# A planner that is told TensorE's measured times, and first loads that are let through one behind the other

## The chip, the cores and the metric

The kernel runs on one core of a Trainium2 chip. The metric is the device time of one execution in microseconds; the kernel before takes 572.33 us (median of 3 runs, 572.28 to 572.41). The core has TensorE (PE: matmuls into PSUM, and PEld, its weight loads), VectorE (DVE), ScalarE (ACT), GpSimd (POOL) and SyncE (SP), which here issues every DMA. Each engine works through its own list of instructions in order and waits on semaphores for the others.

## The reference

Two decoder layers on x of 256 positions by 1024 channels, all in float32. Layer 0 mixes positions with a gated MLP, layer 1 with attention (one block of 256 keys, so it is plain causal attention with a relative-position bias); after each stands a gated ConvFFN of width 2816, and each sub-layer ends in a LayerNorm of alpha * x + f(x).

```python
def chunked_gmlp(x, w_in, ln_g, ln_b, w_s, b_s, w_out):
    z = jax.nn.gelu(x @ w_in)
    u, v = jnp.split(z, 2, axis=-1)
    v = layer_norm(v, ln_g, ln_b)
    ...
    sv = jnp.einsum('gts,bnsgc->bntgc', w, v) + b_s.T[None, None, :, :, None]
    return (u * sv.reshape(B, S, GMLP_WIDTH)) @ w_out

def conv_ffn(x, w_up, conv_w, conv_b, w_down):
    h = x @ w_up
    ...
    g, val = jnp.split(hc, 2, axis=-1)
    return (jax.nn.gelu(g) * val) @ w_down

def reference(...):
    for i in range(DEPTH):
        ...
        x = layer_norm(DN_ALPHA * x + y, ln_mix_g[i], ln_mix_b[i])
        y = conv_ffn(x, f_w_up[i], f_conv_w[i], f_conv_b[i], f_w_down[i])
        x = layer_norm(DN_ALPHA * x + y, ln_ffn_g[i], ln_ffn_b[i])
    return x
```

## The kernel before

Weights stream from HBM in chunks of 128 rows by 2048 columns (1 MB): the v half of the gMLP's input projection (a_v, 4 chunks), its u half (a_u, 4), a_out (4), f_up0 (22), f_dn0 (11), b_v (4), b_qk (8), b_o (4), f_up1 (22) and f_dn1 (11). A float32 product is made of three faster ones: each weight w is split into whi (ACT copies it into the rounded type float32r) and wlo = w - whi (DVE subtracts), the activations likewise into the two parts of xt, and PE adds up x_hi*whi, x_hi*wlo and x_lo*whi. `prep(i)` loads chunk i into one of two buffers `raw` and splits it; `whi` and `wlo` are rings of ten halves, so five chunks are split ahead (CHUNKS = 5). Once a chunk's matmuls are recorded, `spent` calls `prep` for the chunk five further on.

The first stage, a_v in `gmlp()`, needs per step k (128 of the 1024 input channels) half a chunk of a_v and the columns k of the transposed input, which come as "xT" and are split into xt. Its 8 steps have 12 matmuls of 512 columns each: two blocks of positions t, two halves of 512 outputs p, three products. Steps 0 to 3 take both t in turn; then t = 0 does k = 4 to 7, and t = 1 after it. The table FIRST cuts the first two chunks' loads into pieces with a rank, and XFIRST gives the pieces of xT theirs; a rank is the load's place in SP's order, 0 to 8. Chunks 2 and 3 have none and reuse the buffers of chunks 0 and 1.

```
    FIRST = {0: [(0, 512, 0), (512, 1024, 2), (1024, 2048, 4)], 1: [(0, 1024, 6), (1024, 2048, 7)]}
    XFIRST = ((0, 1, 1), (1, 1, 3), (2, 2, 5), (4, 4, 8))
```

After a_v come gelu and a LayerNorm of v (`stats`, `scaled`), then a_u with the mixing matmuls `spatial(g)` laid between its own, then a_out.

No order is written out by hand. Every operation is recorded in a `Plan` with a cost in ns, its inputs and outputs. `emit` computes due times back from PE's list and then plays the engines against each other with these costs (line 122 on): PE's main work ("bulk") keeps the recorded order; its other work ("fill": transposes, spatial, the attention's scores and products) goes in as soon as the plan says that its inputs are there. The engines' lists are what this play gives. The costs of a matmul stand in `mms` (line 322) and those of transposes in line 333: 216 ns for a float32r matmul of 512 columns, 109 for one of 256.

`project_out` does a_out, f_dn and b_o: their last TAIL = 6 steps go position block by position block, and within t = 0 half by half (p0 with all its steps, then p1). When a half is complete DVE adds it to x (`add`, line 612) and takes statistics; then the mean, the power on POOL and one scaling per half (line 351) make the normalised x that PE transposes (line 332) for the next stage, while the matmuls of t = 1 go on.

## Time and profile before

| | |
|---|---|
| median of 3 runs | 572.33 us |
| the profiled execution: its time, its span | 571.2 us, 569.5 us |
| PE busy | 556.1 us (98%) |
| DVE busy | 464.3 us (82%) |
| ACT busy | 359.2 us (63%) |
| DMA | 110.9 MB, mean 195 GB/s |

The span runs from the first to the last instruction of the profiled execution; the run's time has 1.7 us around it, and the median lies 1.1 us above this one run. An engine is busy while it executes. Matmuls are pipelined, so their busy times overlap and their pace is read from the distance between their starts. The waits say which engine waited for which, and the chain of waits follows the work back from the last instruction.

### The profile page before, as it was taken

The numbers are of one execution on the slowest core, as the hardware profiler recorded it, in microseconds if no ns is written. First come the engines' busy times: TensorE is split into PE (matmuls) and PEld (weight loads), VectorE is DVE, ScalarE is ACT, GpSimd is POOL, SyncE is SP. The second block draws the span as 40 slices with busy tenths as digits, with TensorE's granted clock in tenths as the row PEclk, the third lists the DMA queues.
The fourth block names the chain that finished last, engine by engine and source line by source line (L and its number), as shares of the span: only waits on it lengthen the run. The fifth ranks groups of instructions, "written<-read, shape, count | busy, mean of one in ns | idle before, by whom it ended". The sixth has DMA issues, their size and how long they took to land.

```text
span 569.5 us, 8289 instructions
## 1 busy us (share of the span) xinstructions
PE 556.1 (98%) x3098; PEld 474.9 (83%) x3098; DVE 464.3 (82%) x873; ACT 359.2 (63%) x652; POOL 11.5 (2%) x17
## 2 busy tenths in 40 slices
PE   6999999999999999999999999999999999999994
PEld 4799888888888878888888877788888888888884
DVE  5598989999999997467958988579989999996526
ACT  5555558776777686335578877377777767775300
POOL 0020010000000000001000000010000000000001
PEclk9999999999999999999999999999999999999998
DMA  7897435547554577742665653506455556566302
GB/s 266 330 361 283 181 146 182 189 153 279 171 211 155 216 229 266 270 165 74 222 221 185 194 210 115 222 2 221 156 218 219 201 174 218 195 242 229 147 1 74
DMA packets 20132, 110.92 MB, mean 195 GB/s; under 512 B 2251, under 2 KB 6268, under 8 KB 7676
## 3 DMA queue, kind: packets, MB, share of 16 engines
q1 hardware_dynamic: 20092, 110.39, 54.2%
q8 instruction: 24, 0.39, 0.3%
q14 instruction: 16, 0.13, 0.1%
HBM read 109.31 MB, written 1.07 MB: 194 GB/s over the span
## 4 chain that ended last, share of the span: by engine, by line
PE 95%; DMA 2%; DVE 1%; SPq 0%; ACT 0%; issue 0%; DVEq 0%
PE twos L326 52%; PE bank L326 41%; DMA raw<-in_a_v 2%; PE bank L332 1%; PE twos L332 1%; DVE wlo L344 0%; DVE x L348 0%; SPq L355 0%; ACT whi L338 0%; DVE stat L494 0%; DVEq L966 0%; DVE stat L497 0%; DVE stat L499 0%; DVE xt L344 0%
## 5 line engine op out<-in xcount | busy, mean ns | idle before, releaser
L344 DVE TENSOR_TENSOR wlo<-raw,whi 128x1024 fp32r<-128x1024 f32 (+1 forms) x212 | 228.2, 1099 | 33.7 <-ACT whi L338 32.8
L338 ACT ACTIVATE whi<-raw 128x1024 fp32r<-128x1024 f32 (+1 forms) x212 | 194.8, 954 | 55.1 <-DMA raw<-in_f_dn 21.3
L326 PE MATMUL twos<-xt,whi 128*128 128x512 f32 x640 | 222.2, 394 | 0.0
L326 PE MATMUL twos<-xt,wlo 128*128 128x256 f32 x640 | 177.3, 277 | 0.0
L326 PEld LDWEIGHTS twos<-xt,whi 128*128 128x128 f32 x640 | 120.0, 188 | 27.8
L326 PE MATMUL bank<-whi,rr 128*128 128x512 f32 x432 | 135.5, 391 | 0.0
L326 PEld LDWEIGHTS twos<-xt,wlo 128*128 128x128 f32 x640 | 120.1, 188 | 0.1
L326 PEld LDWEIGHTS bank<-whi,rr 128*128 128x128 f32 x432 | 81.1, 188 | 17.9 <-issue 1.0
L326 PE MATMUL bank<-wlo,rr 128*128 128x512 f32 x216 | 84.0, 389 | 0.0
L326 PE MATMUL bank<-xt,whi 128*128 128x256 f32 (+1 forms) x256 | 71.0, 348 | 0.0
L348 DVE SCALAR_TENSOR_TENSOR ff<-ff,convc 128x254 f32<-128x254 f32 (+1 forms) x160 | 69.6, 478 | 0.3
L338 ACT ACTIVATE ff<-twos 128x512 f32<-128x512 f32 (+1 forms) x56 | 30.8, 565 | 47.9 <-PE twos L326 44.8
L326 PE MATMUL bank<-xt,wlo 128*128 128x256 f32 x192 | 54.0, 281 | 0.0
L326 PEld LDWEIGHTS bank<-xt,whi 128*128 128x128 f32 x256 | 44.0, 190 | 6.8 <-issue 1.0
L326 PEld LDWEIGHTS bank<-wlo,rr 128*128 128x128 f32 x216 | 40.6, 188 | 8.0
L338 ACT ACTIVATE ff<-ff,convc 128x256 f32<-128x256 f32 x80 | 45.6, 592 | 1.9 <-DVE ff L344 1.2
L344 DVE TENSOR_TENSOR ff<-twos,ff 128x512 f32<-128x512 f32 (+1 forms) x48 | 30.9, 645 | 15.3 <-ACT ff L338 13.0
L326 PE MATMUL twos<-whi,xt 128*128 128x512 f32 x128 | 42.1, 396 | 0.0
L338 ACT ACTIVATE ff<-bank,lncol 128x128 f32<-128x128 f32 x48 | 18.8, 458 | 29.1 <-PE bank L332 29.1
L326 PEld LDWEIGHTS bank<-xt,wlo 128*128 128x128 f32 x192 | 36.4, 190 | 0.0
L348 DVE SCALAR_TENSOR_TENSOR x<-x,bank 128x512 f32<-128x512 f32 x16 | 11.0, 686 | 25.0 <-PE bank L326 25.0
L326 PEld LDWEIGHTS twos<-whi,xt 128*128 128x128 f32 x128 | 24.1, 188 | 4.8
(71 smaller groups left out, 489.1 us busy)
## 6 DMA issues: line engine op xcount, KB each, us to landing
raw<-in_f_up SPq DMA_DIRECT2D x44, 1024.0 KB, 4.8
raw<-in_f_dn SPq DMA_DIRECT2D x22, 1024.0 KB, 4.9
raw<-in_b_qk SPq DMA_DIRECT2D x8, 1024.0 KB, 4.9
lnrow<-in_lnrow SPq DMA_DIRECT2D x5, 1024.0 KB, 6.7
raw<-in_a_u SPq DMA_DIRECT2D x4, 1024.0 KB, 5.1
raw<-in_a_out SPq DMA_DIRECT2D x4, 1024.0 KB, 5.0
raw<-in_b_v SPq DMA_DIRECT2D x4, 1024.0 KB, 4.9
raw<-in_b_o SPq DMA_DIRECT2D x4, 1024.0 KB, 5.0
```

The costliest lines, as they stand in the source:

```text
L326: nc.tensor.matmul(o, l, x, start=start, stop=stop)
L332: nc.tensor.transpose(o, x, ident.ap)
L338: plan.op("act", ns, lambda: nc.scalar.activation(o, x, func, **kw), r, w, table=table)
L344: dve(70 + 1.04 * flat(x), lambda: nc.vector.tensor_tensor(o, x, y, op=op), r, w)
L348: lambda: nc.vector.scalar_tensor_tensor(o, x, s, y, op0=op0, op1=op1), r, w)
```

## The change

Five things change.

- The costs that the plan is told: a float32r matmul of 512 columns is 227 ns instead of 216, one of 256 is 120 instead of 109, float32 ones and transposes differ too, and matmuls of 64 rows get a formula of their own. They order the whole kernel's lists anew.
- The first loads: chunks 2, 3 and 4 get ranks as well; chunks 2 and 3 come in halves and have places of their own (in `ff` and in the row buffer `lnrow`), so they no longer wait for chunks 0 and 1 to be split. Ranked loads go out strictly in the order of rank, all before any other.
- Seven transfers of 64 bytes (`hold`) stand in SP's list, each ahead of a load and each reading from a piece loaded two or three pieces earlier. SP cannot pass one until that piece has landed. The table HOLD says which waits for which.
- DVE first writes zeros into 512 columns, and PE multiplies them 8 times into an unused bank (WARM) before its first real matmul. xT is stored so that the columns k of both position blocks lie side by side: the load of one k is 128 rows of 1 KB (before: 256 pieces of 512 bytes), and splits take both blocks at once.
- Step 0 of a_v goes over both t for each product in turn (`first_step`), and in `project_out` the last step of both halves of t = 0 stands behind all others (`todo.sort`).

```diff
@@ -46,6 +46,7 @@
 AHEAD = 12000
+WARM = 8
 
@@ -154,6 +155,7 @@
         nb = 0
+        ranked = sorted((o for o in ops if o.rank is not None), key=lambda o: -o.rank)
 
@@ -167,6 +169,8 @@
                     c = [x for x in c if x[1].fill or (nb < len(bulk) and x[1] is bulk[nb])]
+                if e == "sp" and ranked:
+                    c = [x for x in c if x[1] is ranked[-1]]
                 if not c:
@@ -186,6 +190,8 @@
             cand[e].remove(pick)
+            if o.rank is not None:
+                ranked.remove(o)
             if o.eng == "pe" and not o.fill:
@@ -319,7 +325,9 @@
             n = flat(x)
-            ns += max(107.0, n / 2.4) + 2.5 if l.dtype == F32R else (218.0 if n <= P else n / 0.6 + 5)
+            ns += n / 2.4 + 13.4 if l.dtype == F32R else n / 0.6 - 25.0
+        if min(seq[0][1].shape) < P:
+            ns = 0.68 * ns + 200.0
 
@@ -330,7 +338,7 @@
                 nc.tensor.transpose(o, x, ident.ap)
-        plan.op("pe", 110.0 * len(seq), emit, list(r) + [ident], w, True)
+        plan.op("pe", 60.0 + 93.0 * len(seq), emit, list(r) + [ident], w, True)
 
@@ -379,15 +387,33 @@
 
-    FIRST = {0: [(0, 512, 0), (512, 1024, 2), (1024, 2048, 4)], 1: [(0, 1024, 6), (1024, 2048, 7)]}
+    FIRST = {0: [(0, 512, 0), (512, 1024, 2), (1024, 2048, 4)], 1: [(0, 1024, 6), (1024, 2048, 7)],
+             2: [(0, 1024, 9), (1024, 2048, 10)], 3: [(0, 1024, 11), (1024, 2048, 12)], 4: [(0, 2048, 13)]}
+
     XFIRST = ((0, 1, 1), (1, 1, 3), (2, 2, 5), (4, 4, 8))
+
+    EARLY = {2: lambda: place("ff", HALF + KT * S, CH), 3: rowring.new}
+
+
+    HOLD = {5: (0, 0), 7: (0, SUB), 9: (1, 0), 10: (1, SUB), 11: (2, 0), 12: (2, SUB), 13: (3, 0)}
+    scratch = sb.tile([1, 16 * len(HOLD)], F32, name="scratch")
+    loaded, gates = {}, []
+
+    def hold(rank):
+        i, at = HOLD[rank]
+        g = Buf(scratch[:, 16 * len(gates):16 * len(gates) + 16])
+        load(g.ap, loaded[i].ap[:1, at:at + 16], [g], [(loaded[i], [at // 256])], nbytes=64, rank=rank - 0.5)
+        gates.append(g)
 
         name, c = stream[i]
-        raw = raws.new()
+        raw = loaded[i] = EARLY.get(i, raws.new)()
         cuts = FIRST.get(i, [(0, CH, None)])
         for s, e, rank in cuts:
-            load(raw.ap[:, s:e], a[name][c, :, s:e], [(raw, range(s // 256, e // 256))], rank=rank)
+            if rank in HOLD:
+                hold(rank)
+            load(raw.ap[:, s:e], a[name][c, :, s:e], [(raw, range(s // 256, e // 256))],
+                 rank=rank)
         subs = []
@@ -428,20 +454,34 @@
     xT32 = place("ff", HALF, KT * S)
-    xv32 = xT32.ap.rearrange("p (t k c) -> p t k c", t=NT, k=KT)
 
     def load_xt(k, n, rank):
-        load(xv32[:, :, k:k + n, :], a["xT"][:, :, k:k + n, :], [(xT32, [(t, j) for t in range(NT) for j in range(k, k + n)])],
-             rank=rank)
-        for t in range(NT):
-            parts = [(t, j) for j in range(k, k + n)]
-            split((xh, parts, xt_view(xh)[:, t, k:k + n, :]), (xl, parts, xt_view(xl)[:, t, k:k + n, :]),
-                  (xT32, parts, xv32[:, t, k:k + n, :]), by="dve" if k == 0 else "act")
+        def cut(j, m):
+            return slice(j * S, (j + m) * S), [(t, i) for t in range(NT) for i in range(j, j + m)]
+
+        sl, parts = cut(k, n)
+        if rank in HOLD:
+            hold(rank)
+        load(xT32.ap[:, sl], a["xT"][:, sl], [(xT32, parts)], rank=rank)
+        for j in range(k, k + n, 2):
+            m = min(2, k + n - j)
+            sl, parts = cut(j, m)
+            hv, lv = (both[:, j:j + m, o:o + S] for o in (0, S))
+            xv = xT32.ap[:, sl].rearrange("p (k x) -> p k x", k=m)
+            split((xh, parts, hv), (xl, parts, lv), (xT32, parts, xv), by="dve" if k == 0 else "act")
+
+
+    zeros, idle = place("rr", 0, HALF), bank()
+    dve(480, lambda: nc.vector.memset(zeros.ap.bitcast(F32), 0.0), (), [zeros])
+    for _ in range(WARM):
+        mms([(idle.ap, zeros.ap[:, :P], zeros.ap, True, True)], [zeros], [idle], fill=True)
 
     prep(0)
-    for k, n, rank in XFIRST:
-        load_xt(k, n, rank)
-    for i in range(1, CHUNKS):
+    for x in XFIRST[:3]:
+        load_xt(*x)
+    prep(1)
+    load_xt(*XFIRST[3])
+    for i in range(2, CHUNKS):
         prep(i)
@@ -617,11 +657,14 @@
                 mine += ends
-            for p in mine:
-                for k in range(start, nk):
-                    if t == 0 and k == nk - 2:
-                        plan.tick(AHEAD)
-                    step(t, k, [p], first=start if p in ends else 0)
+
+            todo = [(p, k) for p in mine for k in range(start, nk)]
+            if t == 0:
+                todo.sort(key=lambda x: x[1] == nk - 1)
+            for p, k in todo:
+                if t == 0 and k == nk - 2:
+                    plan.tick(AHEAD)
+                step(t, k, [p], first=start if p in ends else 0)
             if t == NT - 1:
@@ -643,7 +686,23 @@
         v = []
+
+        def first_step():
+
+            (hi, lo), x = sub("a_v", 0, 0), [at(0, t) for t in range(NT)]
+            for p in range(2):
+                for part, w in ((0, hi), (1, hi), (0, lo)):
+                    for t in range(NT):
+                        o, n, b = pieces[t][p]
+                        mms([(b.ap, x[t][part], w.ap[:, o:o + n], part == 0 and w is hi, False)],
+                            x[t][2][part:part + 1] + [(w, range(o // 256, (o + n) // 256))], [b])
+            plan.tick()
+
         for k, t in order:
+            if k == 0:
+                if t == 0:
+                    first_step()
+                continue
             rows_step(pieces[t], *at(k, t), *sub("a_v", k // 2, k % 2), k == 0, k == KT - 1)
@@ -918,7 +977,7 @@
         "x": f(x.reshape(NT, P, D).transpose(1, 0, 2)),
-        "xT": f(x.reshape(NT, P, KT, P).transpose(3, 0, 2, 1)),
+        "xT": f(x.reshape(NT, P, KT, P).transpose(3, 2, 0, 1).reshape(P, KT * S)),
         "a_v": by_rows(w_in[:, D:]),
```

The names in the following lists: raw_85 and raw_86 are the two load buffers, ff the scratch area (it holds xT and, in the changed kernel, chunk 2), lnrow_90 the row buffer, bank_107 to bank_110 PSUM banks, x_88 the positions of t = 0 and x_89 those of t = 1.

SP's list from its first DMA, before:

```order
L355 DMA raw_85<-in_a_v 128x512
L355 DMA ff<-in_xT 128x2x128
L355 DMA raw_85<-in_a_v 128x512
L355 DMA ff<-in_xT 128x2x128
L355 DMA raw_85<-in_a_v 128x1024
L355 DMA ff<-in_xT 128x2x256
L355 DMA raw_86<-in_a_v 128x1024 x2
L355 DMA ff<-in_xT 128x2x512
L355 DMA raw_85<-in_a_v 128x2048
L355 DMA raw_86<-in_a_v 128x2048
L355 DMA lnrow_90<-in_lnrow 128x2048
```

And now, from the fifth DMA on (the four ahead of it are the same pieces):

```order
L363 DMA raw_85<-in_a_v 128x1024
L363 DMA scratch<-raw_85 1x16x1
L363 DMA ff<-in_xT 128x512
L363 DMA raw_86<-in_a_v 128x1024
L363 DMA scratch<-raw_85 1x16x1
L363 DMA raw_86<-in_a_v 128x1024
L363 DMA ff<-in_xT 128x1024
L363 DMA scratch<-raw_86 1x16x1
L363 DMA ff<-in_a_v 128x1024
L363 DMA scratch<-raw_86 1x16x1
L363 DMA ff<-in_a_v 128x1024
L363 DMA scratch<-ff 1x16x1
```

The list goes on with `scratch` ahead of each half of chunk 3 (into lnrow_90) and ahead of a_u's first chunk; the LayerNorm rows, which stood right behind chunk 3, now stand behind two chunks of a_u.

DVE's list where a_out ends for t = 0, before (wlo_80 to wlo_82 are halves of f_up0's chunks):

```order
L348 SCALAR_TENSOR_TENSOR x_88<-x_88,bank_107 128x512
L494 BN_STATS stat_93<-x_88 128x6
L344 TENSOR_TENSOR wlo_80<-raw_85,whi_70 128x512 x2
L344 TENSOR_TENSOR wlo_81<-raw_86,whi_71 128x512
L348 SCALAR_TENSOR_TENSOR x_88<-x_88,bank_108 128x512
L494 BN_STATS stat_93<-x_88 128x6
L497 BN_AGGR stat_93<-stat_93 128x2
L499 TENSOR_SCALAR stat_93<-stat_93 128x1
L344 TENSOR_TENSOR wlo_81<-raw_86,whi_71 128x512
L351 TENSOR_SCALAR x_88<-x_88,stat_93 128x512 x2
```

And now:

```order
L356 SCALAR_TENSOR_TENSOR x_88<-x_88,bank_108 128x512
L356 SCALAR_TENSOR_TENSOR x_88<-x_88,bank_109 128x512
L534 BN_STATS stat_93<-x_88 128x6 x2
L537 BN_AGGR stat_93<-stat_93 128x2
L539 TENSOR_SCALAR stat_93<-stat_93 128x1
L352 TENSOR_TENSOR wlo_82<-raw_86,whi_72 128x512
L359 TENSOR_SCALAR x_88<-x_88,stat_93 128x512 x2
```

Both additions and both statistics now stand together behind t = 0's last matmuls; the first pair has left its place among the splits.

The third place is DVE's list behind a_v, where the LayerNorm of v ends (stat_91 is t = 0, stat_92 is t = 1). Before:

```order
L348 SCALAR_TENSOR_TENSOR ff<-ff,stat_91,lnrow_90 128x512
L499 TENSOR_SCALAR stat_92<-stat_92 128x1
L348 SCALAR_TENSOR_TENSOR ff<-ff,stat_92,lnrow_90 128x512
L348 SCALAR_TENSOR_TENSOR ff<-ff,stat_91,lnrow_90 128x256
L344 TENSOR_TENSOR wlo_77<-raw_85,whi_67 128x1024
L348 SCALAR_TENSOR_TENSOR ff<-ff,stat_92,lnrow_90 128x256
```

And now:

```order
L356 SCALAR_TENSOR_TENSOR ff<-ff,stat_91,lnrow_90 128x512
L539 TENSOR_SCALAR stat_92<-stat_92 128x1
L356 SCALAR_TENSOR_TENSOR ff<-ff,stat_92,lnrow_90 128x512
L356 SCALAR_TENSOR_TENSOR ff<-ff,stat_91,lnrow_90 128x256
L356 SCALAR_TENSOR_TENSOR ff<-ff,stat_92,lnrow_90 128x256
```

The split of a_u's third chunk has moved behind the LayerNorm. On PE, the first spatial matmuls stood behind 72 matmuls of a_u and stand behind 54 now, the second group right with them.

## Rows read from the trace of the kernel before

**Rows 1.** The page: the span, and the busy time of each engine over it.

```profile
span 569.5 us, 8289 instructions
PE 556.1 (98%) x3098; PEld 474.9 (83%) x3098; DVE 464.3 (82%) x873; ACT 359.2 (63%) x652; POOL 11.5 (2%) x17
```

**Rows 2.** The waits of PE over the whole span: its line, what it waited for, us in total, times, the longest.

```profile
PE bank L326 <- DVE xt L361: 4.9, 1, 4.9
PE bank L326 <- DVE wlo L344: 0.8, 1, 0.8
```

**Rows 3.** The chain of waits, first 32 us: start, us, what.

```profile
3.15 5.63 DMA raw<-in_a_v
...
8.80 0.64 ACT whi L338
...
9.47 0.56 DVE wlo L344
...
10.08 0.69 DVE wlo L344
...
10.79 7.21 DMA raw<-in_a_v
...
18.03 1.07 ACT whi L338
...
19.12 1.24 DVE wlo L344
...
20.40 11.70 PE bank L326 x53
```

**Rows 4.** The timeline of PE: start, us, operation, count. A count of 2 stands for two matmuls with one start shown.

```profile
4.92 0.77 PE L326 MATMUL bank<-whi,xt 128*128 128x512 f32 x1 [4.92 <-DVE xt L361]
...
7.64 1.05 PE L326 MATMUL bank<-whi,xt 128*128 128x512 f32 x2
8.50 0.63 PE L326 MATMUL bank<-wlo,xt 128*128 128x512 f32 x1
8.92 1.05 PE L326 MATMUL bank<-whi,xt 128*128 128x512 f32 x2
...
10.20 0.98 PE L326 MATMUL bank<-whi,xt 128*128 128x512 f32 x2
...
11.03 0.40 PE L326 MATMUL bank<-wlo,xt 128*128 128x512 f32 x1
...
11.26 0.63 PE L326 MATMUL bank<-whi,xt 128*128 128x512 f32 x2
...
16.06 0.62 PE L326 MATMUL bank<-whi,xt 128*128 128x512 f32 x2
16.51 0.39 PE L326 MATMUL bank<-wlo,xt 128*128 128x512 f32 x1
16.74 0.62 PE L326 MATMUL bank<-whi,xt 128*128 128x512 f32 x2
...
31.23 0.40 PE L326 MATMUL bank<-xt,whi 128*128 128x256 f32 x2
...
39.86 1.06 PE L326 MATMUL twos<-ff 128*128 128x128 f32 x8
```

**Rows 5.** DMAs issued in the first 22 us: what, how many, KB each, median us from issue to landing.

```profile
raw<-in_a_v SPq DMA_DIRECT2D x3, 512.0 KB, 6.6
...
raw<-in_a_v SPq DMA_DIRECT2D x2, 256.0 KB, 3.4
```

**Rows 6.** The same for 110 to 190 us, where DMA has pauses.

```profile
raw<-in_f_up SPq DMA_DIRECT2D x13, 1024.0 KB, 4.8
```

**Rows 7.** Stretches (from:to, us) with busy time (instructions) of PE, PEld, DVE, ACT, POOL, then PEclk, the DMA engines' share and GB/s.

```profile
1.80:5.30 3.50, 0.38 (x1) 0.29 (x1) 0.75 (x4) 0.91 (x2) 0.00 (x0) 1.00 0.69 206
...
9.00:15.50 6.50, 6.50 (x26) 5.26 (x25) 5.82 (x10) 5.03 (x10) 0.00 (x0) 1.00 1.08 384
```

**Rows 8.** SP's own timeline: each row the issue of DMAs.

```profile
3.15 0.60 SPq L355 DMA_DIRECT2D raw<-in_a_v  x1
...
14.63 0.43 SPq L355 DMA_DIRECT2D lnrow<-in_lnrow  x1
```

**Rows 9.** The costliest groups of the first 31.2 us by shape: count, busy us, mean ns of one, idle before.

```profile
L344 DVE TENSOR_TENSOR wlo<-raw,whi 128x512 fp32r<-128x512 f32 x8 | 5.3, 689 | 1.4 <-ACT whi L338 1.3
...
L361 DVE CAST xt<-ff 128x128 fp32r<-128x128 f32 x2 | 0.4, 222 | 3.6 <-DMA ff<-in_xT 3.6
```

**Rows 10.** The timeline of DVE where a_out ends for t = 0, and PE's transposes behind it.

```profile
71.63 0.69 DVE L348 SCALAR_TENSOR_TENSOR x<-x,bank 128x512 f32<-128x512 f32 x1 [0.87 <-PE bank L326]
72.35 0.69 DVE L494 BATCH_NORM_STATS2 stat<-x 128x6 f32<-128x512 f32 x1
...
74.52 1.00 DVE L351 TENSOR_SCALAR x<-x,stat 128x512 f32<-128x512 f32 x2 [0.44 <-POOL stat L500]
...
75.51 1.03 PE L332 MATMUL bank<-ident,x 128*128 128x128 f32 x8
```

**Rows 11.** The same at the ends of f_dn0 and of b_o.

```profile
259.88 1.00 DVE L351 TENSOR_SCALAR x<-x,stat 128x512 f32<-128x512 f32 x2 [0.73 <-POOL stat L500]
...
261.18 1.03 PE L332 MATMUL bank<-ident,x 128*128 128x128 f32 x8
...
371.44 1.00 DVE L351 TENSOR_SCALAR x<-x,stat 128x512 f32<-128x512 f32 x2 [0.73 <-POOL stat L500]
...
372.75 1.03 PE L332 MATMUL bank<-ident,x 128*128 128x128 f32 x8
```

**Rows 12.** DVE's last scaling of v ahead of the first spatial matmuls.

```profile
37.55 0.48 DVE L348 SCALAR_TENSOR_TENSOR ff<-ff,stat,lnrow 128x256 f32<-128x256 f32 x1
```

**Rows 13.** Stretches of the attention (b_qk), columns as in rows 7, and DVE at the end of the kernel.

```profile
306.00:362.00 56.00, 56.00 (x379) 44.56 (x377) 47.68 (x164) 44.27 (x122) 0.00 (x0) 1.00 0.50 173
...
553.55 0.69 DVE L348 SCALAR_TENSOR_TENSOR x<-x,bank 128x512 f32<-128x512 f32 x1 [2.66 <-PE bank L326]
...
561.94 0.42 DVE L348 SCALAR_TENSOR_TENSOR x<-x,twos 128x256 f32<-128x256 f32 x1 [1.28 <-PE twos L326]
```

## The prediction

> **What bounds the kernel now.** The page comes first: PE is busy for 556 of 569.5 us [rows 1], so it sets the end wherever it doesn't wait. So I read PE's waits next: two in the whole span, 4.9 us for the first data and 0.8 us for a split of weights [rows 2]. The third reading is the chain of waits, which names what stood before those waits: SP's fifth load, issued at 3.15 and landed at 8.78, then ACT's and DVE's splits of it, then chunk 2, which could be issued only at 10.79, when its buffer was free, and landed at 18.0; its splits end at 20.36, and from 20.40 on the chain is PE [rows 3]. So everything that can be won lies ahead of 20.4 us, and what can be lost lies anywhere behind.
>
> The fourth reading is PE's timeline. a_v begins at 4.92, a_u at 31.23 [rows 4]: 26.3 us for 96 matmuls. From 7.64 to 8.92 three matmuls start, 427 ns each: 512 columns at 1.2 GHz. From 16.06 to 16.74 it is 227 ns each, the level of 2.4 GHz. The slow pace holds from the first matmul to 11.03, the fast one from there [rows 4]; the granted clock reads 1.00 throughout [rows 7], so only the distances tell. At the fast pace 96 matmuls are 21.8 us: 4.5 us are lost in this stage. By the same rows step 0 (12 matmuls) ends at 10.63, and from there 84 x 0.2267 = 19.0 would end at 29.67; the missing 1.56 us is mostly the stop at 19.1 to 20.4 for chunk 2.
>
> **The change part by part.** I follow a_v's end from 31.23.
>
> *The fifth load* (second half of chunk 0, needed by step 1) lands 5.6 us after its issue, though a quiet 1 MB load takes 4.8 [rows 3, 6]. Ahead of it stand four pieces; in 1.8 to 5.3 us the DMA engines are busy for 0.69 and move 206 GB/s, while later, full, they move 384 [rows 7]. So small pieces, not bytes, hold it up, and the change halves the pieces of xT (1 KB instead of 2 x 512 B per row); later loads mixing in are held back too. Bounds: 8.8 (nothing gained) and 3.15 + 3.4 = 6.55 (as a 256 KB load of these first ones [rows 5]). I take 8.0, nearer to the first, since the bytes ahead of it and their order stay.
>
> *Warm matmuls.* The zeros are one DVE write of 512 columns, not in the trace; a cast of 128 takes 222 ns and a subtraction of 512 takes 689 [rows 9]; so PE starts at 0.9 + 0.2 to 0.7, about 1.4. Eight matmuls at 427 ns end at 4.8, just as the first real one can start (4.92). Before, the pace rose 6.1 us after the first matmul [rows 4]; from 1.4 that gives 7.5. Step 0 in its new order: two matmuls by 5.8, then a wait until DVE has made x_lo (cast 4.55 to 4.85, one split of 0.69, x_lo of 0.4: 6.0), then 3.5 slow and 6.5 fast ones: 9.0 instead of 10.63. If the zeros don't count it stays 10.6; if the pace rose at once, 8.3.
>
> *Step 1* needs the fifth load split: by rows 3 ACT 0.64, DVE 0.56, with gaps: the second product can start at landing + 1.3, so the step at landing + 1.1 = 9.1. That is just behind step 0's end: from there on data, not the clock, is the limit. 9.1 + 19.04 = 28.1, if nothing waits again.
>
> *The holds.* The wait for chunk 2's buffer goes (landing 18.0, start 20.4), and another comes: a half is issued only after one landed two halves earlier, plus about 0.5 us for the tiny transfer (SP's issues take 0.43 to 0.60 [rows 8]). Queued behind a hold are all later loads, so also a_u and the LayerNorm rows. The last half (step 7) hangs on the fifth load by three such links: landing + 3 x 0.5 + 3T, with T from issue to landing of 512 KB. PE wants it, split (1.4 more), at landing + 1.1 + 55 matmuls x 0.2267 = landing + 13.6. So PE waits 3T - 10.7 us once T is over 3.55. No row shows T alone: 512 KB took 6.6 in the crowded start, 256 KB 3.4, a quiet 1 MB 4.8 [rows 5, 6]. Between the last two T = 3.9, which I take, with two in flight at most: a wait of 1.0. With 3.4 it is 0, with 4.8 it is 3.7. a_v then ends at 28.1 + 1.0 = 29.1 instead of 31.23: 2.1 us won. The Trainium skill's page "DMA: Bandwidth & Descriptors" (section "Anatomy of one DMA") fits a transfer as 2.0 us plus bytes at 436 GB/s, found on another path than SP's: an estimate of 3.2 for 512 KB, 4.4 for 1 MB, where this trace has 4.8; by it no hold would bite, and the sum would be 1.0 better.
>
> *Behind a_v.* The LayerNorm of v ended 38.03 - 31.23 = 6.8 us after a_v [rows 4, 12]; PE wanted it after 72 matmuls of 120 ns, at 39.86, 8.6 us after a_v's end, and now after 54, 6.5. DVE no longer splits 1.2 us of weights in between, so 5.6 to 6.8 against 6.5: 0 to 0.3, I take 0.1. The row load for it is issued later, at about 22 behind a_u's two chunks, and has until 32: covered unless the holds run late.
>
> *The sorted last step.* In a_out, f_dn0 and b_o the first half's addition and statistics stood under the second half's matmuls. Now both additions and both statistics follow the end: the first addition ends where the second began, so one statistics pass, 0.72 us, is added [rows 10]. In a_out the two scalings of 1.00 us ended at 75.0 and 75.52, the transposes began at 75.51 and reach the second half 0.44 later: moved by 0.72 they make PE wait 0.2 to 0.3. In f_dn0 and b_o the margin is 0.8 for the first and 0.74 for the second half [rows 11]: 0 to 0.1 each. At the kernel's end the same delay lies under the 8.4 us between 553.55 and 561.94 [rows 13]. Together I take 0.4; bounds 0.1 and 1.0.
>
> *The costs.* PE's real paces are 227 and 120 ns, so the old plan thought PE 5% too fast in these, and what it took to be just in time had room to spare. That room goes. PE waited for nothing in 541 us, DVE is busy 48 of 56 us in the attention [rows 13], and its real 0.69 for a split of 512 is above the plan's 0.60. Instructions and shapes stay the same. Bounds: -0.3 (some transposes come in one group instead of two) and +2.4 (a tenth of a us at each of the 24 groups of scores, transposes and products in the attention); I take 0, since the distances between scores, transposes and products in PE's list changed both ways.
>
> Sum: 2.1 - 0.1 - 0.4 = 1.6, rounded up to 1.7 for the bounds below zero. The profiled execution, 571.2 us with its 569.5 of span, would be 569.5 with 567.8; the median lies 1.1 higher: 570.6 us.
>
> **Rivals.**
> 1. *Nothing bites.* T under 3.55, a_v ends at 28.1, other losses 0.3: 2.8 won, 569.5. For it: a quiet 1 MB takes only 4.8. Against: two halves share the engines.
> 2. *No change.* The fifth load lands at 8.8 as before and T is 4.2: 8.8 + 1.1 + 19.04 + 1.9 = 30.8, and 0.5 goes behind: 572.4. For it: the pieces ahead carry the same bytes; the halves land late on single engines, as chunk 2 did with 7.2 us from issue to landing.
> 3. *The holds turn the queue into a relay, slower.* Place: SP's list between the fifth load and a_u. It decides from T = 4.4, where 3T - 10.7 plus 0.5 eats the gain; with 4.8 the kernel takes 573.4, with 6.6 (as these loads took in the start) PE waits 9.1 and it is 579. For it: nine more transfers and the queue runs dry between a landing and the next bytes. Against: at most two halves share the engines, while the 6.6 was measured with five in flight. The Trainium skill ("DMA: Bandwidth & Descriptors", section "Bandwidth") advises transfers of 1 MB and more, which speaks against the halves; the 4.8 for a quiet 1 MB against two times T agrees.
> 4. *The tighter plan makes PE wait later.* Price 2.4 in the attention, net 0.8 slower: 573.1. Against: PE's list there has the old distances within 1 us.
> 5. *The zeros don't raise the pace.* Step 1 starts at 10.6, but the holds then no longer bite: a_v ends at 29.7, and with 0.5 behind the kernel takes 571.3.
>
> **How the numbers follow.** My case (1.2 to 2.6 us won) has 0.44, rival 1 0.16, rival 2 0.18, rival 3 0.10, rival 4 0.05, rival 5 0.07. A change of 0.2% (1.14 us) is what a measurement of this kernel can tell. Faster: 0.44 + 0.16 and a little of rival 5: 0.62; slower: most of rivals 3 and 4, 0.13; the same: 0.25. The range runs from rival 1 with the early pace (568.8) to rival 3 near T = 4.7 (573.2).
>
> **What would show it.** a_u's first matmul at about 29 instead of 31.2; matmuls 427 ns apart from about 1.4 and 227 from 7.5; the fifth load landed at 8.0; SP waiting for landings of a_v between 8 and 19; PE waiting under 1 us for the last half; the a_out transposes waiting 0.2 to 0.3 for DVE. I am wrong if PE waits over 2 us in a_v for halves (T), if step 1 starts at 10 or later, or if PE's waits in the attention add up to more than 1 us.

## The result and the profile after

Six runs of the changed kernel took 575.3 to 582.4 us, median 578.1; six of the kernel before beside them 571.0 to 573.1, median 572.3. The ratio is 1.0118 (95% interval 1.0095 to 1.0141): slower by 1.2%, where I had forecast 570.6. The changed kernel also scatters over 7 us, the kernel before over 2. The profiled execution of the changed kernel is its slowest, 582.4 us, so what it loses is the upper end.

The page of the changed kernel, its span and PE, and the chain of waits by engine:

```profile
span 580.7 us, 8328 instructions
PE 564.9 (97%) x3106; PEld 476.8 (82%) x3106; DVE 462.8 (80%) x876; ACT 362.6 (62%) x656; POOL 10.1 (2%) x17
...
PE 66%; DVE 15%; DMA 13%; ACT 3%; issue 2%; SPq 1%; POOL 0%; DVEq 0%; ACTq 0%
```

The span is 11.2 us longer than in [rows 1], and PE is "busy" for 8.8 us of that; 3.8 us are the eight matmuls on zeros, the rest must be matmuls that stand farther apart. PE's waits over the whole span, which answer to [rows 2]:

```profile
PE bank L334 <- ACT whi L346: 2.3, 3, 0.8
PE bank L334 <- DVE nhalf L447: 1.5, 1, 1.5
PE twos L334 <- DMA ff<-in_rel_bias: 1.2, 1, 1.2
PE twos L334 <- DVE ff L356: 0.9, 1, 0.9
PE twos L334 <- DVE ff L352: 0.8, 2, 0.5
PE bank L334 <- DVE wlo L352: 0.7, 3, 0.2
PE bank L340 <- DVE x L359: 0.7, 1, 0.7
```

Two rows have become seven. The first, three times for ACT's split, is new; the second is the wait ahead of the matmuls on zeros, which now stands where the 4.9 us for the first data stood. PE's timeline [rows 4] shows where PE stops:

```profile
1.52 3.78 PE L334 MATMUL bank<-rr 128*128 128x512 f32 x8 [1.52 <-DVE nhalf L447]
5.10 1.71 PE L334 MATMUL bank<-whi,xt 128*128 128x512 f32 x4
6.64 0.63 PE L334 MATMUL bank<-wlo,xt 128*128 128x512 f32 x2
...
8.50 0.40 PE L334 MATMUL bank<-whi,xt 128*128 128x512 f32 x1
...
20.03 0.50 PE L334 MATMUL bank<-whi,xt 128*128 128x512 f32 x1 [0.78 <-ACT whi L346]
...
22.98 0.50 PE L334 MATMUL bank<-whi,xt 128*128 128x512 f32 x1 [0.80 <-ACT whi L346]
...
25.82 0.50 PE L334 MATMUL bank<-whi,xt 128*128 128x512 f32 x1 [0.68 <-ACT whi L346]
...
33.28 0.40 PE L334 MATMUL bank<-xt,whi 128*128 128x256 f32 x2
```

The start does what it should: zeros from 1.52, full pace (some 230 ns from one matmul to the next instead of 427) from 6.64 (11.03 before), step 1 from 8.50. Then PE stops three times, 2.9 us apart, and a_u begins at 33.28 instead of 31.23. SP's timeline tells what it stops for:

```profile
2.65 0.43 SPq L363 DMA_DIRECT2D raw<-in_a_v  x1
...
7.61 0.50 SPq L363 DMA_DIRECT2D scratch<-raw  x1
...
16.40 0.50 SPq L363 DMA_DIRECT2D scratch<-ff  x1
...
27.12 0.33 SPq L363 DMA_DIRECT2D lnrow<-in_lnrow  x1
```

A tiny transfer (scratch) can be issued once the half that it reads has landed: the fifth load, issued at 2.65, had landed by 7.61. The chain of waits [rows 3] now runs through such links, half after half, down to a_u:

```profile
11.07 5.31 DMA ff<-in_a_v
...
16.40 0.50 SPq L363
...
16.95 5.33 DMA lnrow<-in_a_v
...
22.29 0.50 SPq L363
...
22.84 8.00 DMA raw<-in_a_u
```

The DMA list of 0 to 24 us gives the time from issue to landing of these 512 KB:

```profile
ff<-in_a_v SPq DMA_DIRECT2D x2, 512.0 KB, 5.3
lnrow<-in_a_v SPq DMA_DIRECT2D x2, 512.0 KB, 5.2
```

That is T, the time from issue to landing of half a chunk, which I had taken as 3.9. To see where the rest goes I set the starts of the same matmuls of both traces against each other (the median over the matmuls of 10 us; plus is later than before). In the profiled execution PE is 1.8 us ahead at 10 to 20, 2.05 behind at 30 to 40, 5.1 behind at 80 to 90, 8.5 at 210 to 220, 9.0 at 380 to 390 and 11.25 at 510 to 520. So the stops in a_v (3.8 us) are a third of it. The last 2.2 us fall in the last wide stage (f_up1), where PE waits for nothing. Two windows of 110 us show it, the kernel before first, columns as in [rows 7]:

```profile
392.00:502.00 110.00, 110.00 (x636) 96.19 (x635) 102.73 (x176) 83.49 (x140) 0.00 (x0) 1.00 0.55 195
```

```profile
402.00:512.00 110.00, 110.00 (x624) 95.36 (x623) 106.03 (x182) 86.56 (x142) 0.00 (x0) 1.00 0.59 212
```

PE is busy throughout, at a granted clock of 1.00 in both, and does 624 matmuls instead of 636 in the same time. This stage is one stream of pairs, a matmul of 512 columns and one of 256. Between stops a pair takes 347 ns in one trace and 353 in the other, for some 320 pairs: 2.1 us. I had no such thing on my list.

### The profile page after: what moved, and what is told of

Its sections match the earlier page's. It is cut to its first block, busy times and chain, and to the rows that moved or that the text cites. A ratio compares the mean times of both kernels' runs of the same rounds, so it can differ in the third digit from the quotient of the medians.

```text
span 580.7 us, 8328 instructions
## 1 busy us (share of the span) xinstructions
PE 564.9 (97%) x3106; PEld 476.8 (82%) x3106; DVE 462.8 (80%) x876; ACT 362.6 (62%) x656; POOL 10.1 (2%) x17
## 4 chain that ended last, share of the span: by engine, by line
PE 66%; DVE 15%; DMA 13%; ACT 3%; issue 2%; SPq 1%; POOL 0%; DVEq 0%; ACTq 0%
PE twos L334 32%; PE bank L334 31%; DVE wlo L352 7%; DMA raw<-in_f_up 5%; DVE ff L356 3%; DMA raw<-in_a_out 2%; DVE ff L352 2%; ACT whi L346 2%; DMA raw<-in_a_v 1%; DMA raw<-in_a_u 1%; PE bank L340 1%; PE twos L340 1%; DMA lnrow<-in_a_v 1%; DMA ff<-in_a_v 1%; DMA raw<-in_f_dn 1%
## 5 line engine op out<-in xcount | busy, mean ns | idle before, releaser
L352 DVE TENSOR_TENSOR wlo<-raw,whi 128x1024 fp32r<-128x1024 f32 (+1 forms) x210 | 224.6, 1089 | 55.6 <-ACT whi L346 55.3
L346 ACT ACTIVATE whi<-raw 128x1024 fp32r<-128x1024 f32 (+1 forms) x210 | 191.9, 946 | 88.4 <-PE bank L334 26.2
L334 PE MATMUL twos<-xt,whi 128*128 128x512 f32 x640 | 225.6, 398 | 0.8 <-DVE ff L352 0.8
L334 PE MATMUL twos<-xt,wlo 128*128 128x256 f32 x640 | 179.1, 280 | 0.0
L356 DVE SCALAR_TENSOR_TENSOR ff<-ff,convc 128x254 f32<-128x254 f32 (+1 forms) x160 | 67.7, 479 | 0.3 <-ACT ff L346 0.3
L346 ACT ACTIVATE ff<-ff,convc 128x256 f32<-128x256 f32 x80 | 43.9, 591 | 14.0 <-DVE ff L352 14.0
```

What stands on the lines that cost most here:

```text
L334: nc.tensor.matmul(o, l, x, start=start, stop=stop)
L346: plan.op("act", ns, lambda: nc.scalar.activation(o, x, func, **kw), r, w, table=table)
L352: dve(70 + 1.04 * flat(x), lambda: nc.vector.tensor_tensor(o, x, y, op=op), r, w)
L356: lambda: nc.vector.scalar_tensor_tensor(o, x, s, y, op0=op0, op1=op1), r, w)
```

## The experiments

One table for all kernels: median us; ratio to the kernel before timed beside them (572.3 beside the change, 571.2 to 571.8 beside the others); PE's lag behind the trace of before at three places (one execution each; the kernel before's own start moves too, since edits that don't touch it show -1.5 to +0.6 at 34); and ns a pair between stops in the two wide stages, from the same one execution.

| label | us | ratio, 95% | at 34 | at 85 | at 515 | ns a pair |
|---|---|---|---|---|---|---|
| the change | 578.1 | 1.0095-1.0141 | 2.0 | 5.1 | 11.2 | 347 and 353 by turns, 353 |
| e1_costs | 575.6 | 1.0048-1.0105 | 0.2 | 1.0 | 3.6 | 353, 347 |
| e2_oldcosts | 578.0 | 1.0083-1.0131 | 1.8 | 2.2 | 7.3 | 353, 353 |
| e3_nohold | 573.2 | 1.0025-1.0070 | -0.4 | -0.3 | 0.6 | 347, 347 |
| e4_neither | 574.7 | 1.0028-1.0069 | -0.8 | -0.8 | 3.5 | 353, 353 |
| e5_pairs | 571.7 | 0.9994-1.0030 | 0.5 | 0.5 | 1.2 | 348, 348 |
| e6_light | 573.0 | 1.0015-1.0042 | -3.0 | -3.1 | 1.2 | 353, 353 |
| e7_light_pairs | 569.4 | 0.9952-0.9979 | -2.9 | -2.1 | -1.1 | 348, 348 |
| e8_nowarm | 573.9 | 1.0028-1.0057 | -1.7 | -0.6 | 3.6 | 353, 353 |
| e9_nosort | 573.9 | 1.0024-1.0057 | -2.5 | -2.0 | 3.5 | 353, 353 |
| e10_sort | 571.6 | 0.9970-1.0017 | -1.5 | -1.5 | 4.2 | 353, 347 |
| e11_entry | 569.0 | 0.9934-0.9971 | -2.4 | -2.4 | -2.3 | 347, 347 |
| e12_after_pairs | 575.6 | 1.0043-1.0095 | 2.1 | 4.2 | 5.4 | 348, 348 |
| e13_light_costs | 570.9 | 0.9974-1.0015 | -1.6 | 0.1 | 3.5 | 347 then 353, 347 |
| e14_costs_entry | 576.1 | 1.0044-1.0097 | 0.6 | 1.8 | 6.3 | 353, 353 |
| e15_after_entry | 578.8 | 1.0096-1.0143 | 0.8 | 2.8 | 7.6 | 353, 353 |
| e16_holds_entry | 577.9 | 1.0079-1.0122 | 2.0 | 2.0 | 7.1 | 353, 353 |
| e17_pairs_light_costs | 571.5 | 0.9988-1.0015 | -1.2 | 0.1 | 1.6 | 348, 348 |
| e18_pairs_holds | 574.3 | 1.0031-1.0068 | 1.7 | 1.9 | 3.2 | 348, 348 |

### One part at a time: costs and tiny transfers

New costs on the kernel before (e1), old costs in the changed kernel (e2, the same lines turned round), no tiny transfers (e3), and e3 with the old costs (e4):

```diff
-            ns += max(107.0, n / 2.4) + 2.5 if l.dtype == F32R else (218.0 if n <= P else n / 0.6 + 5)
+            ns += n / 2.4 + 13.4 if l.dtype == F32R else n / 0.6 - 25.0
+        if min(seq[0][1].shape) < P:
+            ns = 0.68 * ns + 200.0
...
-        plan.op("pe", 110.0 * len(seq), emit, list(r) + [ident], w, True)
+        plan.op("pe", 60.0 + 93.0 * len(seq), emit, list(r) + [ident], w, True)
```

```diff
-    HOLD = {5: (0, 0), 7: (0, SUB), 9: (1, 0), 10: (1, SUB), 11: (2, 0), 12: (2, SUB), 13: (3, 0)}
-    scratch = sb.tile([1, 16 * len(HOLD)], F32, name="scratch")
+    HOLD = {}
+    scratch = sb.tile([1, 16], F32, name="scratch")
```

> The kernel before with nothing but the new costs of matmuls and transposes in the plan. Theory H (the held halves turn around in 5.3 us instead of the 3.9 that I took; what is late behind them is late for that reason): the costs are worth nothing, 572.3 within 0.6. Theory C (the new costs put DVE's and ACT's work in an order that makes PE wait in the wide feed-forward stages, where DVE has the least room): the losses that the trace of the changed kernel shows behind 130 us, about 3.4 us up to the end of the attention, come with the costs alone: 575 to 576.

> The changed kernel with the old costs in the plan, all else kept. Theory H: the 3.8 us at 20 to 30 us and the 2.4 us at 40 to 50 us stay, a_v ends near 33.3, and the time stays at 577 to 578. Theory C: the losses behind 130 us go, 574 to 575, with a_v's end still near 33.3.

> The changed kernel without the seven tiny transfers; the strict order, the halves, the warm-up and the new costs stay. Theory H: PE does not wait for the halves, a_v ends at 28.5 to 30, the 2.4 us at 40 to 50 us go too, and the time falls by about 6 us to 571 to 573. Theory C: only the 3.8 us of the start go (574 to 575), since what comes behind a_v is the costs' doing.

> The changed kernel without the tiny transfers and with the old costs. Theory H: as without the transfers alone, 571 to 573. Theory C: both losses go and the 1.8 us that PE was ahead at 19 us stay: 570.0 to 571.0.

e1 came out as theory C said (575.6), but not for its reason: 2.1 of the 3.6 us in its trace are the first wide stage at 353 ns a pair, with no wait in it. e2 kept the full loss, with both wide stages at 353. e4 missed both theories (574.7), it too with both at 353, and e3's 573.2 lies just above theory H. So medians alone mislead here; the lag at 34 us does not: with seven tiny transfers it is +1.8 to +2.0, without -0.4 to -0.8. The transfers cost; the rest had to be taken apart from the pace first.

### Two tiny transfers instead of seven, and the zeros

```diff
-    HOLD = {5: (0, 0), 7: (0, SUB), 9: (1, 0), 10: (1, SUB), 11: (2, 0), 12: (2, SUB), 13: (3, 0)}
+    HOLD = {5: (0, 0), 7: (0, SUB)}
```

with the old costs; e8 has `WARM = 0` as well. (The first of the two reads the very first piece, five loads earlier, the second the fifth load.)

> The changed kernel with the old costs and only the first two of the seven tiny transfers (those ahead of the rest of xT and of chunk 1's second half). Theory H: the fifth load still lands near 7.6, so PE is 1.5 to 1.8 us ahead of the kernel before at 14 us, and with chunks 2 and 3 let loose as before nothing stalls after that: at 33 us PE is 1.0 to 1.8 ahead. The time is 569.5 to 570.5 with both wide stages at 347 ns a pair, 2 us more for each that runs at 353. Its rival (a queue with eight loads in flight serves the early ones late whatever is held at the start): PE waits again between 12 and 22 us, the lead at 33 us is under 0.8, the time 570.5 to 572 and upward.

> The same as the one with two tiny transfers, without the eight matmuls on zeros. Theory: the granted full pace comes as late as in the kernel before, near 11 us instead of 6.6, step 0 ends at about 10.4 instead of 8.5, and PE at 33 us is 1.2 to 1.9 later than with them: the time 0.8 to 1.9 higher. Rival (the matmuls on zeros are hidden, since the fifth load sets the end of the start anyway): PE at 33 us within 0.4.

PE is 3.0 us ahead at 34, more than expected, and both wide stages at 353 take 4.3 us: 573.0, 0.5 below what the expectation's clause on the pace gives for two such stages. What the two transfers bring is the fifth load: here it has landed by 7.73, in e4, without any, at 10.05, later than the 8.78 of the kernel before. In e3, also without any, it lands at 10.44, as the chain of waits there has it:

```profile
2.65 7.79 DMA raw<-in_a_v
```

Windows of 12 to 18 and 18 to 24 us (the last two columns are the DMA engines' share and GB/s), the changed kernel and then e6_light:

```profile
12.00:18.00 6.00, 5.96 (x26) 4.41 (x26) 3.87 (x7) 3.46 (x6) 0.00 (x0) 1.00 0.72 246
18.00:24.00 6.00, 3.97 (x13) 2.20 (x14) 2.70 (x5) 2.30 (x4) 0.00 (x0) 1.00 0.58 182
```

```profile
12.00:18.00 6.00, 6.00 (x28) 4.96 (x27) 4.38 (x8) 4.52 (x8) 0.00 (x0) 1.00 1.02 394
18.00:24.00 6.00, 6.00 (x28) 4.87 (x27) 3.85 (x7) 5.21 (x9) 0.00 (x0) 1.00 0.99 396
```

With two halves in flight and a trip from landing to the next issue in between, the DMA engines stand idle for 28 to 42% of the time; let loose, the same queue moves twice as much in 18 to 24 us. Without the zeros PE is 1.3 us less far ahead at 34 and the median 0.8 higher; step 0 then ends at 10.4:

```profile
4.98 2.22 PE L332 MATMUL bank<-whi,xt 128*128 128x512 f32 x4 [4.98 <-ACT whi L344]
...
10.41 0.43 PE L332 MATMUL bank<-whi,xt 128*128 128x512 f32 x1
10.68 0.40 PE L332 MATMUL bank<-wlo,xt 128*128 128x512 f32 x1
10.92 0.62 PE L332 MATMUL bank<-whi,xt 128*128 128x512 f32 x2
```

### The pace of the wide stages

Twos of equal width, in the kernel before (e5) and in e6_light (e7):

```diff
-        for k in range(KT):
...
-            mms([(o, hi.ap[:, ks], both[:, k], k == 0, False),
-                 (o[:, S:], lo.ap[:, ks], both[:, k, :S], False, k == KT - 1)],
...
+        for k0 in range(0, KT, 2):
+            two = [(k, slice(k * P, (k + 1) * P)) for k in (k0, k0 + 1)]
...
+            mms([(o, hi.ap[:, ks], both[:, k], k == 0, False) for k, ks in two] +
+                [(o[:, S:], lo.ap[:, ks], both[:, k, :S], False, k == KT - 1) for k, ks in two],
...
```

> The kernel before, with the wide feed-forward stages' matmuls issued as two of 512 columns, then two of 256, instead of 512 and 256 by turns. The traces so far show two paces of one and the same stream of 512 and 256 by turns: 347 ns a pair (231 + 116) in both wide stages of the kernel before, 353 ns (236 + 117) in the last one of the changed kernel and in some stages of the other runs, held for a whole stage of 320 pairs, 2.0 us. Theory P (the pace is something that the alternation of the two widths can fall into): with equal widths side by side the stages run at 347 ns a pair (227 + 120) in every execution: the median within 0.5 of 571.3, the spread smaller than the 4.8 us of the kernel before. Theory Q (the pace belongs to the execution, not to the order): the same spread as before, and stages with 353 ns a pair in some executions.

> The same with the wide stages' matmuls two of 512 and two of 256. Theories P and H together: 569.5 to 570.5 in all executions. Theory Q: 569.5 to 575 by execution.

Both wide stages run at 348 in both kernels. On the kernel before that buys nothing (its two stages were at 347), and its runs still spread over 4.2 us (the kernel before's over 4.6), so the narrower spread of theory P did not come there. On e6_light it buys 3.6 us: 569.4, all twelve runs within 1.2 us. This beats both kernels. Next, is it the sorted last step that brings the slower pace? e9 is e6_light with the two lines of the sort taken out, e10 the kernel before with them:

```diff
+            if t == 0:
+                todo.sort(key=lambda x: x[1] == nk - 1)
```

> The kernel with two tiny transfers and the old costs, without the sorted last step of the first row tile. Theory S (the sorted step is what brings the wide stages, which follow it and the second tile, to the pace of 353 ns a pair): both stages run at 347 ns a pair and the 3.1 us of lead at 33 us stay: 568.0 to 569.0. Rival E (the pace falls out of nanoseconds at a stage's entry, which the sorting has no part in): at least one stage at 353, 570.2 or more.

> The kernel before with the sorted last step alone. Theory S: both wide stages at 353 ns a pair, 575 to 576. Rival E: not tied to it; with both stages at 347 ns a pair 571.3 within 0.5, since the trace of the kernel with the old costs and no tiny transfers shows PE neither nearer nor farther behind a_out's end than ahead of it.

No: e9 runs both stages at 353 without it. e6 and e10, which have the sort, also lose nothing between 34 and 85 us. (e10's profiled execution, its slowest of twelve, has one wait of 1.9 us in the attention that no other trace has.) Last, the twos at each wide stage's entry alone, in e6_light (`by` is a new argument of `cols_apart`, the number of pairs laid side by side):

```diff
-                cols_apart(b, j * HALF, h, l, *sub(name, i, j))
+                cols_apart(b, j * HALF, h, l, *sub(name, i, j), by=2 if (i, j) == (2, 0) else 1)
```

> The kernel with two tiny transfers and the old costs, with the matmuls in twos of equal width in the first half of the first step of each wide stage alone (8 pairs of 320). If the pace is set at a stage's entry and then holds (theory E), this can turn it: at least one stage runs at 347 ns a pair to its end, 568.2 to 571.0. If something else sets it throughout (the order of what runs beside it, say), the pairs behind the first eight go on at 353: 572.5 to 573.2.

569.0, ten runs within 1.1 us, both stages at 347 to their end, with eight pairs of some 320 changed. PE's timeline in the last wide stage, e6_light and then e11_entry; all rows between are pairs of the same form:

```profile
439.96 0.40 PE L332 MATMUL twos<-xt,whi 128*128 128x512 f32 x1
440.19 0.28 PE L332 MATMUL twos<-xt,wlo 128*128 128x256 f32 x1
...
442.08 0.40 PE L332 MATMUL twos<-xt,whi 128*128 128x512 f32 x1
```

```profile
439.71 0.40 PE L332 MATMUL twos<-xt,whi 128*128 128x512 f32 x1
439.94 0.28 PE L332 MATMUL twos<-xt,wlo 128*128 128x256 f32 x1
...
441.79 0.40 PE L332 MATMUL twos<-xt,whi 128*128 128x512 f32 x1
```

Six pairs take 2.12 us there and 2.08 here, 353 and 347 ns. So one stream has two paces, and what comes at its entry can turn it, though nothing in the text of the stage differs after that. Nor does anything else: in the two traces every engine has the same operations in the same order, by names and shapes, apart from these entries. The runs of the two kernels don't overlap either (572.2 to 574.4 and 568.7 to 569.7).

### The four combinations at one pace

The twos throughout, with seven tiny transfers and the new costs (e12, the change whole), two and new (e17), seven and old (e18); e7 is two and old.

> The changed kernel whole, with the wide stages' matmuls two of 512 and two of 256. What the pace has no part in must stay: by the trace 2.0 us at a_v's end, 2.4 to 3.1 in a_u and a_out, 3.3 in the first wide stage where DVE is late: 575.5 to 580, and the spread stays above 3 us. If the pace were most of it, 572 to 574.

> Two tiny transfers, the new costs, twos of equal width throughout (with the old costs 569.4). Theory C' (the new costs put VectorE's work on a_u's and a_out's weights later, whatever the loads do: 0.9 to 2.5 us at 40 to 60 us in the traces that have them): 570.3 to 571.9. Rival (they do harm only where loads are late): 569.0 to 569.8.

> Seven tiny transfers, the old costs, twos of equal width throughout. Theory H (five tiny transfers too many cost 4 to 5 us at a_v's end, the costs 1 to 2 more behind it): 573.2 to 574.6, which is 4 to 5 above the kernel with two and 1 to 2 below the changed kernel with twos. Rival (behind late loads the costs don't matter): 575 to 576.

| | old costs | new costs |
|---|---|---|
| two tiny transfers | 569.4 | 571.5 |
| seven | 574.3 | 575.6 |

The five transfers more cost 4.9 us with the old costs and 4.1 with the new; the new costs 2.1 and 1.3. The last is the least sure, since the intervals of e18 and e12 overlap, and the four were timed in three sessions (the kernel before 571.2 to 571.4 in each). Both theories hold beside each other, H with the larger share, and the rival that the costs harm only late loads falls. The first expectation erred in part: the spread fell to 3 us, and the 3.3 us between 85 and 210 were 0.5, so those stalls need not come with the change.

### Runs that did not settle it

Before the four combinations I had tried the entry in twos for the same purpose: on e6_light with the new costs (e13), on the kernel before with them (e14), on the changed kernel (e15) and on it with the old costs (e16).

> Two tiny transfers, the new costs, and the entry of each wide stage in twos (that with the old costs took 569.0). Theory C' (the new costs by themselves cost some stalls, 0.9 at 40 to 50 us and 0.5 in the attention, as in the trace of the kernel before with the new costs alone): 569.8 to 570.5. Rival (they do harm only where loads are late): 568.6 to 569.4.

> The kernel before with the new costs and the entry of each wide stage in twos. Theory C': 1.0 to 1.5 above the kernel before, 572.2 to 572.8, with both wide stages at 347 ns a pair. Rival: within 0.5 of it, so that the 4.4 us that the new costs alone took in their first run were all pace.

> The changed kernel whole, with the entry in twos. Theory: the holds' 2.0 us at a_v's end and 2.4 to 3.1 behind it stay, the pace's 2 us go: 574.5 to 576, with both wide stages at 347 ns a pair where PE does not wait inside them. If the stalls inside the first wide stage (3.3 us in the profiled run of the changed kernel) belong to the change, 577 to 578.

> The changed kernel with the old costs and the entry in twos. If the losses in a_u and a_out need the new costs beside the late loads: 573.5 to 574.5 (1.8 at a_v's end, 0.5 in a_u, 0.6 in the attention, as in the trace with the old costs). If the late loads alone bring them: as the changed kernel whole with that entry, 574.5 to 576.

All four medians lie above what the first theory of each expected, by 0.4 to 3.4 us, and the traces of e14 to e16 have both wide stages at 353: the entry that turned the pace to 347 in e11 leaves e16 where e2 was without it, and in e14 the last stage stands at 353 where e1 had 347. e13 shows the pace turn by itself. PE's timeline in its first wide stage:

```profile
118.55 0.40 PE L334 MATMUL twos<-xt,whi 128*128 128x512 f32 x1
...
120.63 0.40 PE L334 MATMUL twos<-xt,whi 128*128 128x512 f32 x1
...
121.21 0.27 PE L334 MATMUL twos<-xt,wlo 128*128 128x256 f32 x1
121.50 0.50 PE L334 MATMUL twos<-xt,whi 128*128 128x512 f32 x1
121.84 0.28 PE L334 MATMUL twos<-xt,wlo 128*128 128x256 f32 x1
121.96 0.40 PE L334 MATMUL twos<-xt,whi 128*128 128x512 f32 x1
...
124.08 0.40 PE L334 MATMUL twos<-xt,whi 128*128 128x512 f32 x1
```

Six pairs take 2.08 us up to 120.63; the matmuls at 121.21 and 121.50 stand 0.29 and 0.34 ahead of the next ones instead of 0.12 and 0.23; from 121.96 six pairs take 2.12, and so on to the stage's end. Form and order of the matmuls are the same on both sides of that stop of 0.3 us, so the pace is a state that a stream falls into, and a short stop can change it. The changed kernel's own first wide stage shows it both ways: 347 up to 142.6, 353 behind a stop of 0.8 us, 347 again from 155.5 behind one of under 0.1, 353 from 195.0 behind one of 0.5. Two stops of 0.1 us at 166.2 and 171.9 changed nothing, nor did one of 1 us at 138.2 in e13. What decides which state follows I could not show, nor how often a kernel's pace differs from one execution to the next, since each has one trace.

## Why the prediction was wrong

**The fifth load, the zeros, step 1: right, and a little small.** The load landed at 7.61 (I took 8.0), the pace rose by 6.64 (7.5), step 0 ended at 8.50 (9.0), and e6_light, where nothing else bites, was 3.0 us ahead at 34, where I had 3.1 in the sum of 31.23 - 28.1. Rival 5 falls with e8. Of my two reasons for the earlier landing the second is the one that the runs bear out, the later loads held back: with xT's halved pieces but no tiny transfer it landed at 10.05 to 10.44 (e4, e3).

**The holds: the right formula with a wrong T.** This is the step that failed: "Between the last two T = 3.9, which I take". Put the measured 5.3 into 3T - 10.7 and PE waits 5.2; 7.61 + 1.1 + 19.04 + 5.2 is 32.95, and a_u began at 33.28. The rows that bound it were there. For 512 KB at the start [rows 5] had 6.6, measured with five in flight, and I put it aside for two rows of other sizes and other stretches; 5.3 lies midway between it and my 3.9. The nearest row was the quiet 1 MB of [rows 6], 4.8 us: two halves in flight are the same bytes. With it PE would wait 3.7 us. Rival 3 was what happened, and I gave it 0.10; rivals 1 and 2 fall with T. Its own scale, 573.4 at T = 4.8 and 579 at 6.6, gives 575.0 at 5.3; e18, the tiny transfers at a settled pace and with the old costs, took 574.3. By the Trainium skill's fit ("DMA: Bandwidth & Descriptors", section "Anatomy of one DMA"), found on another path than SP's, I had an estimate of 3.2 us; with two halves in flight 5.2 and 5.3 were measured, and the measurement decides. The Trainium skill's advice of transfers of 1 MB and more (same page, section "Bandwidth"), which I had cited for rival 3, is not what these runs test: e6 moves 394 to 396 GB/s with the same halves (and a_u's loads of 1 MB behind them), so it was the waits rather than the size of the halves that took the rate down to 182.

**The costs: "I take 0" was wrong.** They cost 1.3 and 2.1 us at one pace, inside my bounds of -0.3 to +2.4, but for the most part not in the attention, where rival 4 had looked. From 34 to 85 us, in a_u and a_out, the eight traces with the new costs lose 1.5 us on average (0.1 to 3.1), the eleven without 0.3; from 215 to 385 us they lose 0.4 (e10 apart, the others 0.2). The wait for the LayerNorm of v, below, is the part of it that the traces explain. For the rest my reading, which no run tests by itself, is that the old plan's error had left DVE some time.

**Behind a_v.** I took 0.1 for the LayerNorm of v; in the changed kernel PE waits 0.9 us for it. The scaling that it waits for ends at 40.76, 7.5 us after a_v's end, where I had 5.6 to 6.8. It takes the new costs besides: e2, with the old ones, has it as late (7.5 us), but its first spatial matmuls stand behind 63 of a_u's and not 54, and PE does not wait. This wait is in all five traces with the new costs and tiny transfers (0.5 to 1.0 us; e17 has two transfers), in no other:

```profile
PE twos L334 <- DVE ff L356: 0.6, 1, 0.6
```

I had called the row load covered "unless the holds run late". They ran late: it was issued at 27.12, not 22. But it landed at 35.8, and DVE first reads it at 38.90, behind three splits of a_u's weights that end at 36.89: it stayed covered. I took 0.4 for the sorted step; e6 and e10 show 0 up to 85 us, and in the trace of the change alone do the transposes wait, 0.7 us (in e12 they don't). In that trace PE also waits for the load of rel_bias, ahead of which SP stands for 21 us with five loads of f_dn, each waiting for a buffer:

```profile
185.37 21.23 SPq L363 DMA_DIRECT2D raw<-in_f_dn  x5
...
210.20 0.32 SPq L363 DMA_DIRECT2D ff<-in_rel_bias  x1
```

```profile
211.96 0.80 PE L334 MATMUL twos<-ff 33*16 33x384 f32 x2 [1.22 <-DMA ff<-in_rel_bias]
```

That order comes with the new costs and not from the late start: five stand there in e17 and e3 too, which have two tiny transfers and none, and two or three in every trace with the old costs. Of the other traces only e3 and e17 show the wait, 0.3 us.

**What was on no list: the pace.** The sum now reads, from the medians at one pace: start edits with two transfers -2.3 (569.4 - 571.7), five more +4.9, costs +1.3, together 3.9; +2.5 (578.1 - 575.6) for what the twos take from the change, and 0.3 for what they cost the kernel before: 6.7 above its 571.3 in those sessions, 5.8 above the 572.3 that it took in the change's own. The 2.5 are the pace and whatever stops the twos took away with it: between 85 and 215 us the change's trace loses 3.4 us, partly in waits, and e12's 0.6. These runs do not part the two.

## What to carry to other kernels

Price a limit on loads in flight by the rate that it leaves: one landing, one issue and the next landing in a row have to feed the engine that waits. Where the rows leave the time from issue to landing open (here 3.4 to 6.6 us) and the wait goes from 0 to 9 us between them, the sum hangs on that one number, and the range has to cover both ends. Correcting one engine's cost in a planner moves the other engines' work: here it brought the spatial matmuls forward to where DVE was not ready. That DVE's costs should have been corrected with PE's is a guess, which no run tests. Where a change moves PE by some us and no wait shows it, count matmuls in equal windows before and after.

## What the runs showed that I had not expected

A stream of matmuls of 512 and 256 columns by turns ran at either 347 or 353 ns a pair at the same granted clock of 1.00, mostly for whole stages, and kept its pace until a stop or the stage's end. Of seven stops inside the stages of two traces, from under 0.1 to 1 us, four turned it. Each pace is a pattern of distances from one matmul's start to the next that repeats: at 347 it is 231, 113, 232 and 118 ns, two pairs, in the kernel before, at 353 it is 232, 118, 241, 120, 236 and 113, three pairs, the same to 1 ns in e6_light and in the change. A stage's 320 pairs differ by 2.1 us for it, two stages by 4.2, more than most edits here. Twos of equal width ran at 348 ns a pair in all ten wide stages of the five kernels that have them.
